# Row sums of late conditioning columns four products further on, and a fourth slot for mixed token tiles

## The chip, the cores and the metric

The kernel runs on one core of a Trainium2 chip. The metric is the device time of one execution, in microseconds (us). The engines are named as in the profile: PE is TensorE's matmuls and PEld its weight loads, DVE is VectorE, ACT is ScalarE, POOL is GpSimd, SP is the engine that issues most DMAs. Each engine works through its own instructions in order and waits on semaphores where it needs another's result; a queue of DMA issues is named SPq or ACTq.

## The reference

One layer of a bidirectional encoder: 1024 tokens, 1024 features, float32. Cut to what matters:

```python
mod = silu(c) @ w_ada + b_ada                      # six vectors of 1024: sh1 sc1 gt1 sh2 sc2 gt2
h = rms_norm(x, g_norm1) * (1 + sc1) + sh1
qa, ka, va, qb, kb, vb, gates = split(h @ w_in)    # 8 + 12 heads of 64, and two gates of 1024
o_a = neighbourhood_attention(rms(qa), rms(ka), va, rpb)
o_b = softmax-weighted sum of three dilated window attentions of (qb, kb, vb)
gate_a, gate_b = split(sigmoid(gates + b_gate))
x = x + gt1 * ((gate_a * (o_a @ w_proj_a) + gate_b * (o_b @ w_proj_b)) @ w_o)
h2 = rms_norm(x, g_norm2) * (1 + sc2) + sh2
a, up = split(h2 @ w_ffn_in)                       # 2 x 2816
x = x + gt2 * ((silu(a) * up) @ w_ffn_out)
```

The vectors sh1 and sc1 are made at the start. The other four make up 4096 "late" columns of the conditioning, in eight columns of 512: columns 0 to 3 are gt1 and sh2, 4 and 5 are sc2, 6 and 7 are gt2.

## The kernel before

**Precision and products.** Every float32 operand is split into a high and a low part (`hi`, made on ACT; `lo`, made on POOL or DVE), and each product takes three matmuls per step of the contraction: hi x hi, hi x lo, lo x hi (`PASS`). Large products are done in seven instead of eight block products, with mixed (added or subtracted) blocks of weights and of tokens. The mixed token blocks lie in DRAM as `t_d` (`TD` gives the four that are needed: x1, w22, x3, x2) and are loaded back when needed.

**Order.** TensorE's instructions run in the order in which the code writes them. On the other engines a scheduler may change the order; what the code wraps in `pin` keeps its order among the pinned instructions of its engine. Most loads for weights and all loads of mixed token tiles are pinned on SP. A load into a buffer waits, at the head of SP's queue, until the buffer's last reader is through.

**The paired projection (L1146 to L1253).** The input projection is made head pair by head pair (a "unit"). Units 4 to 9 are made two at a time by `pair_units`, which writes a list of blocks, `stream`. A block is one step of a product: three matmuls of 128 x 384. Four blocks make one token tile, four tiles one product, and the seven products p1, x1, p2, x2, x4, x3, w22 of a pair follow one another: 112 blocks for a pair, 336 for the three pairs, from block 192 on. A product starts at block `s`. `when(p, f)` puts a request ahead of block `p`: raw weights are asked for from `s - 29` on, their high parts are made from `s - 14` on, their low parts from `s - 12` on. Products x1, x2, x3 and w22 take their token tiles from `t_d` (`sload`, L1220). Attention for earlier units is put between the blocks by the main loop (L1265 to L1380), about once in seven blocks.

**Buffers of the pair stage.** The high and low parts of weights share one ring of ten buffers (`NHL`, tags hi and lo), and so do two of three mixed token tiles; each request takes the next buffer of the ring, and waits until the request ten places before it has been used up. A weight is used up by the product's fourth token tile. Every third mixed tile goes into a spare buffer, left free of the token tiles (`spare`, the profile calls it hT). Other buffers: `big` is a ring of eight large buffers for attention operands and others; acc2 holds a running sum of the early conditioning columns; rtab holds the rope table of units 0 to 5.

**The late conditioning columns (L342 to L369).** `late_ada` returns a function that does one step each time it is called. Steps 0 to 7 of a column load one 128 x 512 block of `wada2` and add it, scaled by the conditioning, to the column's sum (`acc`) on DVE. One step of the next column then sums over the 128 partitions: four small matmuls with `ones32` (L352), an add of the bias on DVE (L357) and a store to DRAM, `mod_d` (L358). The bias is loaded by SP ahead of the add (L356). One such function, `ada_gate`, does columns 4 and 5 in the late gate stage: it is called once behind each of the 24 products of `gate_group` (L1443 to L1456). The other, `ada_late`, does columns 6 and 7: it is called once in each of the last 20 of 22 passes of the feed-forward stage (L1811 to L1821). The vector gt2 is loaded from `mod_d` behind that stage (L1828).

**After the gate stage** come eight merges (`merge`, L1465), each of 36 matmuls, the product with `w_o`, the feed-forward input (22 passes of `pair_out`) and the feed-forward output (seven products of `prod2`, L1860). Banks of TensorE's results are given out in turns, two for each of four tags.

Of the kernel before, what the change touches and what calls it, by code (L numbers as in the profile page):

```python
# [11 lines left out]
F32R = mybir.dt.float32r  # L12
# [36 lines left out]
def hybrid_layer(ctx: ExitStack, tc: tile.TileContext, x, colp, wada1, wada2, bada2, wqkv, wg, wpa, wpb,  # L49
# [3 lines left out]
    def pool(name, side, **kw):  # L53
        return tc.alloc_tile_pool(name=name, bufs=1, side=side, reuse_waits="tile", **kw)
# [25 lines left out]
    def bank(tag):  # L80
        return ps.tile([128, 512], F32, tag=tag, name="ps_" + tag)
# [33 lines left out]
    def fview(ap):  # L115
        return ap.bitcast(F32)
# [37 lines left out]
    def spare(q, n, dtype=F32R):  # L154
        return (h1p, h1l)[q].tile([128, n], dtype, tag=f"h{q}01" + ("a" if n == 1536 else "b"), bufs=1, name="hT")
# [15 lines left out]
    ap_ = pool("attn", "right")  # L171
# [7 lines left out]
    def big(name, shape=None, dtype=F32):  # L179
        return ap_.tile(shape or wide, dtype, tag="big", bufs=NBIG, name=name)  # L180
# [27 lines left out]
    def unit_load(u, k, keep=False):  # L208
        return wload(wqkv[u, :, k, :], 384, keep)
# [66 lines left out]
    def tok(part, k, t):  # L276
        return hT[part][k // 4, t // 4][0][k % 4][:, t % 4 * 128:t % 4 * 128 + 128]

    rtab = []
# [62 lines left out]
    def late_ada(p, c0, bankf, tile):  # L342
        state, acc = [0], {}

        def step():
            i = state[0]
            state[0] += 1
            c, kk = c0 + i // 8, i % 8
            if kk == 1 and c0 < c <= c0 + 2:
                pm = bankf()  # L350
                for j in range(4):
                    nc.tensor.matmul(pm[32 * j:32 * j + 32, :128], ones32, acc[c - 1][:, 128 * j:128 * j + 128],  # L352
                                     start=True, stop=True)
                br = p.tile([128, 128], F32, tag="br", bufs=1, name="brow")
                bq = bada2[:, (c - 1) * 512:c * 512].rearrange("o (j n) -> (o j) n", j=4)
                nc.sync.dma_start(br, bq[:, None, :].to_broadcast([4, 32, 128]))  # L356
                nc.vector.tensor_add(br, pm[:, :128], br)  # L357
                nc.sync.dma_start(mod_d[(c - 1) * 512:c * 512].rearrange("(j n) -> j n", j=4), br[0:128:32, :])  # L358
            if i >= 16:
                return  # L360
            wa = tile()
            nc.sync.dma_start(wa, wada2[c, :, kk, :])
            if kk == 0:
                acc[c] = p.tile([128, 512], F32, tag="acc", bufs=2, name="acc3")
                nc.vector.tensor_scalar(acc[c], wa, cact[:, 0:1], None, op0=ALU.mult)
            else:
                nc.vector.scalar_tensor_tensor(acc[c], wa, cact[:, kk:kk + 1], acc[c], op0=ALU.mult, op1=ALU.add)

        return step  # L369
# [743 lines left out]
    def when(p, f):  # L1113
        events.setdefault(p, []).append(f)
# [33 lines left out]
    sums, nmix = [], [0]  # L1148
# [26 lines left out]
    def pair_units(ua):  # L1175
        ub = ua + 1
        chain, ch = [], {}
        for nm in PROD:
            s = len(stream)
            r, w = {}, {}  # L1180
            e, k0 = SRC[nm]
            for k in range(4):
                def load(k=k, nm=nm, r=r, e=e, k0=k0):
                    if nm == "x1":
                        if k % 2 == 0:
                            chain.append(big("chain"))
                        ch[k] = chain[-1][:, 512 * (k % 2):512 * (k % 2) + 384]
                        pin(nc.sync.dma_start(ch[k], wqkv[ub, :, k, :]))
                    r[k] = unit_load((ua, ub)[e], k0 + k, True)

                def mix(k=k, nm=nm, r=r):
                    if nm == "x1":
                        nc.gpsimd.tensor_add(ch[k], ch[k], r[k])
                    elif nm == "x2":
                        nc.gpsimd.tensor_sub(ch[k], ch[k], r[k])
                    elif nm == "x4":
                        nc.gpsimd.tensor_sub(r[k], r[k], ch[k])
                    elif nm == "x3":
                        nc.gpsimd.tensor_sub(ch[k], r[k], ch[k])

                def high(k=k, nm=nm, r=r, w=w, s=s):
                    z = ch[k] if nm in ("x1", "x2", "x3") else r[k]
                    w[k] = [wp.tile([128, 512], F32R, tag=g, bufs=NHL, name="w" + g) for g in ("hi", "lo")] + [z]
                    h = nc.scalar.activation(w[k][0][:, :384], z, AF.Copy)  # L1204
                    if s > 192:
                        pin(h)

                def low(k=k, w=w):
                    hi, lo, z = w[k]
                    nc.gpsimd.tensor_sub(lo[:, :384], z, fview(hi[:, :384]))  # L1210

                first = s == 192
                when(s - 29 + 3 * k, load)
                when(s - 19 + 2 * k, mix)
                when(s + (-14, -12, -6, -5)[k] if first else s - 14 + 2 * k, high)
                when(s + (-13, -11, -5, -4)[k] if first else s - 12 + 2 * k, low)
            for t in range(4):
                sm = {}
                if nm in TD:
                    def sload(t=t, nm=nm, sm=sm):  # L1220
                        nmix[0] += 1
                        for q, tag in enumerate(("hi", "lo")):
                            if nmix[0] % 3 == 0:
                                z = spare(q, 512)
                            else:
                                z = wp.tile([128, 512], F32R, tag=tag, bufs=NHL, name="smix")
                            pin(nc.sync.dma_start(fview(z).rearrange("p (k q) -> p k q", k=4), t_d[q, TD[nm], t]))
                            sm[q] = z

                    when(s - 15 + 3 * t if nm in ("x1", "x2", "x3") and t < 3 else s + 4 * t - 8, sload)  # L1230

                def job(k, t=t, nm=nm, w=w, sm=sm):
                    if k == 0:
                        n, i = now
                        sm["pd"] = bank("s" if n % 2 == 0 and n < PAIRED and 0 < i < 4 else "d")
                    pd = sm["pd"]
                    for i, (a, b) in enumerate(PASS):
                        if nm in TD:
                            lhs = sm[a][:, 128 * k:128 * k + 128]
                        else:  # L1240
                            lhs = tok(a, k + (0 if nm == "p1" else 4), t + (4 if nm == "x4" else 0))
                        nc.tensor.matmul(pd[:, :384], lhs, w[k][b][:, :384], start=(k == 0 and i == 0),  # L1242
                                         stop=(k == 3 and i == 2))
                    if k == 3:
                        pair_evac(nm, t, pd, ua, ub)

                for k in range(4):
                    stream.append(lambda k=k, job=job: job(k))
# [3 lines left out]
    for u in (4, 6, 8):  # L1252
        pair_units(u)  # L1253
# [11 lines left out]
    for n in range(6, 92):  # L1265
        u, t = divmod(n, 8)
# [455 lines left out]
    def first_prods(j):  # L1722
        wj[j, "p"] = prod(wj[j, "w11"], blk(0, 0)), prod(wj[j, "w12"], blk(1, 0))

    def first_out(j):
        p1, p2 = wj[j, "p"]
        c11, c12 = cs[j] = [half_tile("e", NE) for _ in range(2)]
        nc.scalar.activation(c12, p1, AF.Copy)
        nc.vector.tensor_add(c11, c12, p2)
# [22 lines left out]
    def first_back(j):  # L1752
        cs[j] = [half_tile("e", NE) for _ in range(2)]
        for n, z in enumerate(cs[j]):
            nc.sync.dma_start(z, e_d[EARLY.index(j) - HELD, n])
# [39 lines left out]
    ada_late = late_ada(adp, 6, prod_bank, lambda: adp.tile([128, 512], F32, tag="wa", bufs=3, name="wa3"))  # L1795
# [15 lines left out]
    for n, j in enumerate(EARLY + tuple(i for k in range(len(EARLY) // 2, HT) for i in (k, k + HT))):  # L1811
        if j not in EARLY[:2]:
            late_weights(j)
        if j in EARLY[HELD:]:
            first_back(j)
        elif j not in cs:
            first_prods(j)
            first_out(j)
        if n >= 2:
            ada_late()  # L1820
        pair_out(j)  # L1821
    for p in tps[::-1] + [ep]:
        p.release()
# [207 lines left out]
```

## Time and profile before

| | us |
|---|---|
| median of 3 runs | 1484.25 |
| lowest and highest run | 1483.57, 1489.17 |
| the profiled execution | 1483.4 |
| its span | 1481.6 |
| PE busy in the span | 1452.2 |
| DVE busy | 1103.0 |
| POOL busy | 731.7 |
| ACT busy | 706.4 |

The profile shows one execution. The page groups instructions by source line, engine and names (the name left of the arrow is written, those right of it are read). A list of waits says for which instruction another one waited, in total, how often and the longest. A timeline gives start, duration, engine, line and operation, and in brackets how long the engine had been idle and who ended that. The windows view gives the busy time of the engines in a stretch and the clock that TensorE was granted, as a share of full speed.

In time the stages lie so: up to about 197 us the start and units 0 to 3, with attention; about 197 to 480 the three pairs; to 608 the first gate products; 608 to 688 the gate groups with `ada_gate`; then the merges, the output projection, the feed-forward input to about 1266 and the feed-forward output.

### The profile page before, as it was taken

Reading aid. Unit: us, or ns where it says so; the run is one execution under the profiler, and the core shown is the slowest. Engines: PE = TensorE matmul, PEld = TensorE weight load, DVE = VectorE, ACT = ScalarE, POOL = GpSimd, SP = SyncE. Lnnn points to the kernel's source line nnn. Section 1 sums busy time; section 2 is a strip of 40 time slices with the busy share of each in tenths; the row PEclk is TensorE's granted clock in tenths of the full one; section 3 lists DMA queues with packets and bytes.
Section 4 is the critical chain, followed back from the end, with each engine's and each line's share of the span. In section 5 each row is a group of like instructions: output and inputs, shape, how many; then the busy total and the mean of one; then the engine's idle time right before and its main releaser. Section 6 shows DMA issues by size and latency. Waiting matters only on the chain.

```text
span 1481.6 us, 24516 instructions
## 1 busy us (share of the span) xinstructions
PE 1452.2 (98%) x8024; PEld 1236.5 (83%) x8024; DVE 1103.0 (74%) x2120; ACT 706.4 (48%) x1771; POOL 731.7 (49%) x706
## 2 busy tenths in 40 slices
PE   8999999998999999989999999999999999999998
PEld 7999999898887777867888888888888888888886
DVE  6788857767588765794877596888777777599568
ACT  5666666656777764545422353332233233354442
POOL 0453476663544464445531402677777775104464
PEclk9999999999999999999999999999999999999999
DMA  9657685756667776955374325345533334898342
GB/s 361 240 175 237 200 276 171 241 181 207 218 185 239 239 247 208 375 159 167 121 247 150 105 87 178 122 152 175 175 102 107 106 109 143 272 349 304 114 157 100
DMA packets 191569, 285.18 MB, mean 192 GB/s; under 512 B 29745, under 2 KB 91857, under 8 KB 190673
## 3 DMA queue, kind: packets, MB, share of 16 engines
q1 hardware_dynamic: 172864, 269.96, 54.6%
q10 hardware_dynamic: 18576, 13.64, 2.8%
q8 instruction: 64, 1.05, 0.3%
q14 instruction: 65, 0.52, 0.1%
HBM read 218.67 MB, written 64.86 MB: 191 GB/s over the span
## 4 chain that ended last, share of the span: by engine, by line
PE 85%; DVE 7%; DMA 3%; ACT 2%; issue 2%; POOL 1%; SPq 0%; ACTq 0%; DVEq 0%; POOLq 0%
PE ps_v L1689 8%; PE ps_d L1689 8%; PE ps_s L1689 7%; PE ps_d L379 7%; PE ps_t L1689 6%; PE ps_d L880 5%; PE ps_d L1242 5%; PE ps_s L1866 3%; PE ps_d L1866 3%; PE ps_t L1866 3%; PE ps_v L1866 3%; PE ps_s L1624 2%; PE ps_d L1624 2%; PE ps_s L1242 2%; PE ps_v L1624 1%
## 5 line engine op out<-in xcount | busy, mean ns | idle before, releaser
L129 ACT ACTIVATE whi<-raw 128x512 fp32r<-128x512 f32 (+2 forms) x265 | 158.1, 609 | 193.9 <-PE ps_s L1866 37.9
L132 DVE TENSOR_TENSOR wlo<-raw,whi 128x512 fp32r<-128x512 f32 (+1 forms) x171 | 152.5, 909 | 47.9 <-ACT whi L129 45.4
L132 POOL TENSOR_TENSOR wlo<-raw,whi 128x512 fp32r<-128x512 f32 (+2 forms) x94 | 129.1, 1382 | 108.9 <-ACT whi L129 104.6
L379 PE MATMUL ps_d<-whi,hT 128*128 128x384 f32 x384 | 101.2, 338 | 0.0
L1639 POOL TENSOR_TENSOR e<-e,c 128x512 f32<-128x512 f32 x44 | 68.8, 1565 | 62.3 <-DVE c L1769 38.2
L1242 PE MATMUL ps_d<-whi,hT 128*128 128x384 f32 x328 | 92.1, 342 | 3.4 <-issue 1.6
L129 ACT ACTIVATE whi<-ws 128x512 fp32r<-128x512 f32 x60 | 37.7, 628 | 119.5 <-DVE ws L1706 81.2
L880 PE MATMUL ps_d<-hT,whi 128*128 128x512 f32 x264 | 84.2, 400 | 0.0
L132 POOL TENSOR_TENSOR wlo<-m,whi 128x512 fp32r<-128x512 f32 x35 | 51.5, 1479 | 51.0 <-ACT whi L129 51.0
L379 PEld LDWEIGHTS ps_d<-whi,hT 128*128 128x128 f32 x384 | 69.6, 188 | 0.6 <-issue 0.6
L1242 PE MATMUL ps_d<-whi,smix 128*128 128x384 f32 x224 | 65.8, 350 | 3.4 <-DMA smix<-t_d 3.1
L1210 POOL TENSOR_TENSOR wlo<-raw,whi 128x384 fp32r<-128x384 f32 x48 | 49.3, 1040 | 36.8 <-ACT whi L1204 32.3
L1637 ACT ACTIVATE e<-e 128x512 f32<-128x512 f32 x44 | 27.4, 630 | 81.8 <-DVE e L1772 56.3
L658 ACT ACTIVATE P<-P,st 128x256 f32<-128x256 f32 (+2 forms) x100 | 45.8, 460 | 38.9 <-DVE st L656 38.9
L379 PE MATMUL ps_d<-wlo,hT 128*128 128x384 f32 x192 | 64.2, 334 | 0.0
L1242 PEld LDWEIGHTS ps_d<-whi,hT 128*128 128x128 f32 x328 | 59.8, 188 | 4.9 <-issue 2.1
L1689 PE MATMUL ps_d<-h2T,whi 128*128 128x512 f32 x200 | 61.6, 389 | 0.0
L1689 PE MATMUL ps_v<-h2T,whi 128*128 128x512 f32 x192 | 59.2, 389 | 0.0
L1689 PE MATMUL ps_s<-h2T,whi 128*128 128x512 f32 x192 | 59.1, 389 | 0.0
L1210 POOL TENSOR_TENSOR wlo<-chain,whi 128x384 fp32r<-128x384 f32 x36 | 38.1, 1071 | 41.8 <-ACT whi L1204 39.4
L132 POOL TENSOR_TENSOR wlo<-gl,whi 128x512 fp32r<-128x512 f32 x30 | 41.2, 1389 | 33.5 <-ACT whi L129 33.4
L1638 DVE TENSOR_TENSOR e<-e 128x512 f32<-128x512 f32 x44 | 42.5, 974 | 17.0 <-ACT e L1637 16.8
(479 smaller groups left out, 4635.5 us busy)
## 6 DMA issues: line engine op xcount, KB each, us to landing
raw<-in_w_dram SPq DMA_DIRECT2D x139, 256.0 KB, 3.3
raw<-in_wqkv_dram SPq DMA_DIRECT2D x116, 192.0 KB, 4.1
ga_d<-e SPq DMA_DIRECT2D x77, 256.0 KB, 2.2
raw<-ga_d SPq DMA_DIRECT2D x77, 256.0 KB, 2.9
smix<-t_d SPq DMA_DIRECT2D x64, 256.0 KB, 3.7
m<-in_w_dram SPq DMA_DIRECT2D x44, 256.0 KB, 5.5
hT<-t_d SPq DMA_DIRECT2D x40, 256.0 KB, 4.3
xt<-in_x_dram SPq DMA_DIRECT2D x16, 512.0 KB, 7.1
```

Of the source, the lines that this page charges most:

```text
L129: h = nc.scalar.activation(hi[:, :n], r, AF.Copy)
L132: (eng or nc.gpsimd).tensor_sub(lo[:, :n], r, fview(hi[:, :n]))
L379: nc.tensor.matmul(pd[:, :384], tok(a, k, t), U.w[k][b][:, :384], start=(k == 0 and i == 0), stop=(k == KT - 1 and i == 2))
L658: nc.scalar.activation(C.P[h][:nq, c], C.P[h][:nq, c], AF.Exp, scale=-1.0, bias=nm, accum_out=sm)
L880: nc.tensor.matmul(pb, w[x][:, k * 128:(k + 1) * 128], b[y][k], start=(k == 0 and q == 0), stop=(k == 3 and q == 2))
L1210: nc.gpsimd.tensor_sub(lo[:, :384], z, fview(hi[:, :384]))
L1242: nc.tensor.matmul(pd[:, :384], lhs, w[k][b][:, :384], start=(k == 0 and i == 0), stop=(k == 3 and i == 2))
L1624: nc.tensor.matmul(pbs[hf], h2T[a][:, k, t * 128:(t + 1) * 128], wow[hf, k][b], start=(n == 0 and (a, b) == PASS[0]), stop=(n == KT - 1 an ...
L1638: nc.vector.tensor_mul(sg, sg, a)
L1639: nc.gpsimd.tensor_mul(sg, sg, up)
L1689: nc.tensor.matmul(pb, w[p][:, k * 128:(k + 1) * 128], b[q][:, k], start=(k == 0 and i == 0), stop=(k == 3 and i == 2))
L1866: nc.tensor.matmul(pb[m], o[0][a][:, m * 128:(m + 1) * 128], o[1][b], start=(k == 0 and i == 0), stop=(k == HT - 1 and i == 2))
```

## The change

Three edits. In `late_ada` the row sum of a column comes at step 5 of the next column instead of step 1, and the upper limit on its column is dropped. `ada_late` is called in all 22 passes instead of the last 20. In `sload` the mixed token tiles have four places in turn instead of three: two in the ring, the spare buffer, and a fourth, which is a `big` buffer in the first pair and the buffers acc2 and rtab in the other two; and all tiles of x1, x2 and x3 are asked for from 15 blocks ahead of their product, three blocks apart (before, the fourth tile 8 blocks ahead of its use), those of w22 12 blocks ahead of their use (before 8).

```diff
@@ -346,7 +346,7 @@
             i = state[0]
             state[0] += 1
             c, kk = c0 + i // 8, i % 8
-            if kk == 1 and c0 < c <= c0 + 2:
+            if kk == 5 and c > c0:
                 pm = bankf()
                 for j in range(4):
                     nc.tensor.matmul(pm[32 * j:32 * j + 32, :128], ones32, acc[c - 1][:, 128 * j:128 * j + 128],
@@ -1218,16 +1218,22 @@
                 sm = {}
                 if nm in TD:
                     def sload(t=t, nm=nm, sm=sm):
+                        slot = nmix[0] % 4
                         nmix[0] += 1
+                        if slot == 3 and ua == 4:
+                            pair = big("smix", [128, 2, 512], F32R)
                         for q, tag in enumerate(("hi", "lo")):
-                            if nmix[0] % 3 == 0:
+                            if slot == 2:
                                 z = spare(q, 512)
+                            elif slot == 3:
+                                z = pair[:, q] if ua == 4 else ap_.tile([128, 512], F32R, tag=("acc2", "rtab")[q], bufs=1,
+                                                                        name="smix")
                             else:
                                 z = wp.tile([128, 512], F32R, tag=tag, bufs=NHL, name="smix")
                             pin(nc.sync.dma_start(fview(z).rearrange("p (k q) -> p k q", k=4), t_d[q, TD[nm], t]))
                             sm[q] = z
 
-                    when(s - 15 + 3 * t if nm in ("x1", "x2", "x3") and t < 3 else s + 4 * t - 8, sload)
+                    when(s + 4 * t - 12 if nm == "w22" else s - 15 + 3 * t, sload)
 
                 def job(k, t=t, nm=nm, w=w, sm=sm):
                     if k == 0:
@@ -1816,8 +1822,7 @@
         elif j not in cs:
             first_prods(j)
             first_out(j)
-        if n >= 2:
-            ada_late()
+        ada_late()
         pair_out(j)
     for p in tps[::-1] + [ep]:
         p.release()
```

## The prediction

> **What bounds the kernel now.** I read the page first, then the windows view over the stages, the list of TensorE's waits, the windows view again around the longest waits (for the granted clock), and the timelines of the queues there.
>
> ```profile
> span 1481.6 us, 24516 instructions
> ...
> PE 1452.2 (98%) x8024; PEld 1236.5 (83%) x8024; DVE 1103.0 (74%) x2120; ACT 706.4 (48%) x1771; POOL 731.7 (49%) x706
> ```
>
> ```profile
> 196.50:480.00 283.50, 272.98 (x2012) 247.75 (x2009) 204.28 (x661) 187.53 (x618) 158.26 (x206) 0.99 0.68 213
> ...
> 608.00:688.00 80.00, 72.62 (x322) 58.88 (x321) 62.28 (x73) 41.45 (x66) 41.49 (x29) 0.96 0.65 227
> ...
> 870.00:1266.00 396.00, 396.00 (x1760) 327.19 (x1759) 304.36 (x361) 125.23 (x214) 252.59 (x176) 1.00 0.41 134
> ```
>
> The columns are length, then busy time of PE, PEld, DVE, ACT and POOL, granted clock, DMA share, GB/s. TensorE is the bound: 98% of the span, and all of 870 to 1266. What can be won is the time in which it stands or runs with a lowered clock. Both show in the two stages that the change touches: the paired projection (196.5 to 480, 10.5 us not busy, clock 0.99) and the late gate products (608 to 688, 7.4 us not busy, clock 0.96).
>
> ```profile
> PE ps_t L352 <- DVE acc L367: 4.6, 1, 4.6
> PE ps_d L1242 <- DMA smix<-t_d: 3.1, 3, 2.5
> PE ps_s L352 <- DVE acc L367: 2.8, 1, 2.8
> ...
> PE ps_s L1242 <- DMA hT<-t_d: 1.7, 1, 1.7
> PE ps_d L1242 <- issue: 1.6, 1, 1.6
> ...
> PE ps_s L1242 <- DVE st L656: 1.0, 1, 1.0
> PE ps_d L1242 <- DVE sx L596: 1.0, 1, 1.0
> ...
> PE ps_d L1242 <- DMA hT<-t_d: 0.6, 1, 0.6
> ```
>
> Total, times, longest. Two row sums (L352) waited 4.6 and 2.8 = 7.4 us for the VectorE sums of their columns. Products on mixed tokens waited 3.1 + 1.7 + 0.6 = 5.4 us for loads ("hT" from t_d is a mixed tile in the spare slot). The rows that name DVE st, DVE sx and issue are waits that no token load ends; the change does not aim at them.
>
> ```profile
> 638.00:641.00 3.00, 0.24 (x5) 1.00 0.78 216
> 641.00:645.00 4.00, 4.00 (x24) 1.00 0.96 253
> 663.00:668.00 5.00, 0.39 (x5) 0.86 0.00 2
> 668.00:671.00 3.00, 3.00 (x14) 0.50 0.01 3
> 671.00:674.00 3.00, 3.00 (x10) 0.59 0.77 273
> ...
> 279.50:282.00 2.50, 2.46 (x10) 0.79 1.02 337
> 282.00:285.50 3.50, 3.50 (x15) 0.66 1.04 352
> ...
> 368.20:374.00 5.80, 5.39 (x22) 0.71 1.04 276
> ```
>
> PE alone; the number behind the count is the clock. A wait can cost twice. After the 4.6 us wait TensorE ran at 0.50 and 0.59 for 6 us; after the 1.7 us wait (ending at 279.5) at 0.79 and 0.66 for 6 us; after the 2.5 us wait (ending at 368.2) at 0.71 for 5.8 us. After the 2.8 us wait (ending at 641) it stayed at 1.00.
>
> **Part A: row sums of the late columns, gate stage.** The step runs once behind each of 24 gate products. Steps 0 to 7 and 8 to 15 build two sums on VectorE; their four row-sum matmuls move from behind products 9 and 17 to behind 13 and 21.
>
> ```profile
> 639.40 1.50 DVE L367 SCALAR_TENSOR_TENSOR acc<-wa,cact,acc 128x512 f32<-128x512 f32 x2
> ...
> 640.96 0.43 PE L352 MATMUL ps_s<-acc,ones 128*32 128x128 f32 x8 [2.76 <-DVE acc L367]
> ...
> 667.17 0.76 DVE L367 SCALAR_TENSOR_TENSOR acc<-wa,cact,acc 128x512 f32<-128x512 f32 x1
> 667.98 0.66 PE L352 MATMUL ps_t<-acc,ones 128*32 128x128 f32 x8 [4.61 <-DVE acc L367]
> ...
> 673.69 0.62 PE L880 MATMUL ps_d<-hT,whi 128*128 128x512 f32 x2
> ...
> 673.89 0.69 DVE L1449 TENSOR_TENSOR sg<-sg,ps_v 128x512 f32<-128x512 f32 x1 [4.57 <-PE ps_v L880]
> ...
> 676.41 0.62 PE L880 MATMUL ps_s<-hT,whi 128*128 128x512 f32 x2
> ```
>
> A product takes 676.41 - 673.69 = 2.72 us. The second sum ended at 667.9. TensorE had come to its row sum at 667.98 - 4.61 = 663.4; four products later is 663.4 + 10.9 = 674.3, less the 2.8 us that the first wait no longer takes: 671.5, 3.6 us after the sum. The first has 638.2 + 10.9 = 649.1 against 640.9. So both waits go: 4.61 + 2.76 = 7.4 us. With the second goes its slow clock: 3 x 0.50 + 3 x 0.41 = 2.7 us. VectorE was 4.57 us idle before 673.89, so its backlog was worked off by 669; it is not a second bound that takes the gain back.
>
> What is moved, and past what: on PE the four matmuls, past four products each; on VectorE the add of the bias, past four adds of those products; on SP the bias load and the store into mod_d, past the loads of the same four steps. POOL and ACT have no part in it.
>
> ```profile
> SPq L358 <- DVE brow L357: 10.8, 1, 10.8
> ```
>
> SP stood 10.8 us before that store, with attention tiles and the first merge weights behind it in the code's order. Behind step 21 the code has only loads for the third merge and later. I cost the store at nothing; the cover is two merges of 36 matmuls, 2.72 / 12 us apart: 16 us. With the cover gone, at most the 10.8 us would come back.
>
> In the feed-forward stage the step starts two passes earlier; row sums come at passes 13 and 21 of 22 instead of 11 and 19.
>
> ```profile
> L367 DVE SCALAR_TENSOR_TENSOR acc<-wa,cact,acc x28: 715/752/2970, 606.2 to 792.3; 128x512 f32<-128x512 f32 x28
> ```
>
> All sums were done by 793, before the stage began at 870, so nothing waits there before or after. The last column's result is stored two passes later (396 / 22 = 18 us each), in the last pass, and is first used after four output products of 11 x 2.72 us. Zero; the cover is 120 us, and without it the cost would be the store's landing, a few us.
>
> **Part B: a fourth slot, earlier requests.** Counted from the code: paired products run in blocks of three matmuls, four blocks to a token tile, seven products of 16 blocks to a pair. Weights and most mixed tiles take turns in a ring of ten buffers; every third mixed tile has the spare slot. A request waits at the head of SP's queue until the buffer's last user is through. Before, the first and second w22 tiles of a pair get their buffer as little as 3 and 6 blocks before use, those in the spare slot 8, and eight of the weight requests stand 5 to 7 blocks for a buffer. After, no weight request stands; x1, x2 and x3 tiles find a buffer long free and are asked 15 to 18 blocks ahead; w22 tiles have 17, 7, 12 and 12 blocks from buffer to use. The last three of these requests still come up to five blocks before their buffer is free; behind them in SP's queue stand the next pair's weights, for which ACT, POOL and then PE would wait.
>
> ```profile
> DMA to landing us min/median/max: 2.9/3.7/6.2
> ```
>
> ```profile
> 356.74 0.33 PE L1242 MATMUL ps_d<-whi,smix 128*128 128x384 f32 x1
> ...
> 362.57 0.35 PE L1242 MATMUL ps_d<-whi,hT 128*128 128x384 f32 x1
> ...
> 368.26 0.41 PE L1242 MATMUL ps_d<-whi,smix 128*128 128x384 f32 x1 [2.52 <-DMA smix<-t_d]
> ```
>
> ```profile
> 363.88 0.32 SPq L466 DMA_DIRECT2D v<-v_d  x1
> 364.29 0.86 SPq L1227 DMA_DIRECT2D smix<-t_d  x2
> ```
>
> The 2.5 us wait: issued at 364.29 behind the load of v, needed at 365.7, landed at 368.2. The new request lies four blocks earlier, ahead of that v load. Its buffer is free at 356.74, where the fourth x3 tile starts: 9 us for 0.9 us of issue and 3.7 of landing. Tightest is the second w22 tile, free one block after 356.74 (357.3) and used at 362.57: 5.3 us against 4.6. With the slowest landing (6.2) it would wait 1.8 us, 5.4 over three pairs; that is the upper bound, and I take zero because the median fits. So the 5.4 us of load waits go, and the lowered clock behind them: 2.5 x 0.21 + 3.5 x 0.34 + 5.8 x 0.29 = 3.4 us.
>
> [...]
>
> The eight weight requests go from standing to not standing; no row above shows PE waiting for them, so I count zero. Next late are the waits for VectorE: without the pauses VectorE falls further behind, and I put back one wait of the size of the DVE rows, 1.0 us; gone altogether, the rows of 1.6 + 1.0 + 1.0 would add 3.6 us of gain.
>
> The new buffers: in the first pair a large attention buffer, later the acc2 and rope-table buffers.
>
> ```profile
> 293.36 0.26 POOL L435 TENSOR_TENSOR rb<-qn,rtab 128x32 f32<-128x32 f32 x1
> ```
>
> That is the rope table's last use, about where the fourth x1 tile of the next pair is asked, 18 blocks before it is needed. Zero.
>
> **Sum.** The profiled execution took 1483.4 us, 1.8 around its span and 0.85 under the median of 1484.25. 1483.4 - 7.4 - 2.7 - 5.4 - 3.4 + 1.0 = 1465.5; against the median 1466.
>
> **Rivals.**
> Clock not tied to the short waits: the low clock at 280 and 370 comes with DMA shares of 1.04, and the 2.8 us wait lowered nothing. 3.4 us stay: 1469.4. Against: it begins right behind each wait. Chance 0.12.
> Only A: waits move to the second w22 tile, or the loads land later in these DMA-full stretches (1.02, 1.04). 1484.25 - 10.1 = 1474. For: 5.3 against 4.6 us. Chance 0.13.
> Only B: in the gate stage VectorE (62.3 of 80 us busy) becomes the bound and late weights take the place of the row sum. 1484.25 - 8.8 = 1475.4. Against: the idle 4.57 us. Chance 0.08.
> It doesn't do what it says: sums end later still and loads stand at the same places: 1484. Chance 0.05.
> Slower: SP stands before w22 loads whose buffers are not free and holds the next pair's weights.
>
> ```profile
> SPq L1227 <- PE ps_d L1242: 56.5, 24, 9.4
> ```
>
> It stood 9.4 us once. By the code the weights behind have 9 blocks from the second w22 buffer to their split, at 283.5 / 336 = 0.84 us a block 7.6 us; less a landing of 3.7 that leaves 3.9. If each pair stood 9.4 us longer there, TensorE would wait 5.5 us and lose 3 more at half clock: 26 us on three pairs, 1466 + 26 = 1492. It decides from 3.9 us on. Against: that stand ends after 5 blocks by the count. Chance 0.04.
> [...]
>
> **How the numbers follow.** My forecast has the other 0.58, its own range 1460 to 1471 (3.6 more gain and 2 of sums read off windows below; the late w22 tile above). A measurement here can tell 0.5%, 7.4 us, so faster is under 1476.8: forecast and first three rivals, 0.91, less 0.09 for the parts of the two near the limit that come out above it: 0.82. Same: 0.05 + 0.09 = 0.14. Slower: 0.04. The range 1460 to 1478 leaves out the last two rivals and a tail, some 0.15.
>
> **What would show it.** L352 without a DVE wait near 640 and 665; clock 1.00 from 608 to 688, that stage 10 us shorter; no DMA smix or hT row above 1 us on L1242; clock 1.00 from 196 to 480, 8 us shorter. Wrong if L352 still waits for acc, if L880 waits for DVE wlo, or if the pair stage keeps its length with SP standing on L1227.

## The result and the profile after

| | before | after |
|---|---|---|
| median, us | 1487.44 | 1472.38 |
| lowest and highest run of after, us | | 1468.93, 1475.41 |
| ratio, 95% interval | | 0.9904 [0.9883, 0.9926] |
| the profiled execution, us | 1483.4 | 1472.6 |

The kernel became faster by 1%. The column of before has six runs, the three of the first table and 1486.83, 1488.05 and 5082.91, so its median is not the 1484.25 of the first table. The ratio is taken from the fast runs alone, without that of 5082.91. The ratio times 1484.25 is 1470, 14.2 us less; the forecast was 1466, 18 us less.

The page of the changed kernel begins so:

```profile
span 1470.8 us, 24489 instructions
...
PE 1449.9 (99%) x8024; PEld 1235.4 (84%) x8024; DVE 1102.8 (75%) x2120; ACT 703.9 (48%) x1771; POOL 732.5 (50%) x706
```

The work is the same on every engine; only TensorE's share of the span rose, from 98 to 99%. Lines from 1224 to 1818 of before are numbered six higher (L1242 is now L1248, L1624 is L1630, L1478 is L1484). The windows of the stages, with the columns of the prediction:

```profile
196.50:480.00 283.50, 274.19 (x2041) 249.85 (x2040) 212.38 (x666) 189.79 (x626) 166.59 (x213) 0.99 0.69 219
608.00:688.00 80.00, 80.00 (x365) 65.45 (x364) 62.96 (x77) 41.19 (x67) 47.30 (x33) 1.00 0.69 234
870.00:1260.00 390.00, 390.00 (x1732) 321.91 (x1731) 295.32 (x347) 122.01 (x213) 253.95 (x177) 1.00 0.42 137
```

The late gate products (608 to 688) run without a gap and at clock 1.00, where before 7.4 us were not busy and the clock was 0.96. The pair stage still has 283.50 - 274.19 = 9.3 us in which TensorE stands, against 10.5, and its clock is again 0.99. The two row sums of the gate stage, in TensorE's timeline, wait for nothing (a wait would stand in brackets behind the row):

```profile
646.37 0.43 PE L352 MATMUL ps_s<-acc,ones 128*32 128x128 f32 x8
668.71 0.43 PE L352 MATMUL ps_t<-acc,ones 128*32 128x128 f32 x8
```

The list of TensorE's waits (total, times, longest), those in the start and of 0.2 left out, and one of 0.6 for VectorE (L477) behind the pair stage:

```profile
PE ps_s L579 <- DVE qk L506: 3.0, 1, 3.0
...
PE ps_d L1630 <- DVE sg L1484: 1.3, 1, 1.3
PE ps_t L605 <- ACT P L597: 1.3, 1, 1.3
PE ps_d L1248 <- DVE hT L1169: 1.1, 1, 1.1
PE ps_t L301 <- DVE PT L678: 1.0, 1, 1.0
PE ps_s L1248 <- DVE st L656: 1.0, 1, 1.0
...
PE ps_d L1248 <- DVE rz L415: 0.9, 1, 0.9
...
PE ps_d L1248 <- DMA smix<-t_d: 0.6, 2, 0.3
PE ps_d L1248 <- PE ps_d L1248: 0.5, 2, 0.3
```

Of 5.4 us of waits for mixed tiles 0.6 are left. In their place stand waits for VectorE: 3.0 + 1.1 + 1.0 + 1.0 + 0.9 = 7.0 us in the pair stage. In the kernel before these were st 1.0 and sx 1.0, shown in the prediction, and four more rows of its list:

```profile
PE ps_d L1242 <- DVE rz L416: 0.4, 1, 0.4
PE ps_s L579 <- DVE qk L506: 0.3, 1, 0.3
PE ps_t L301 <- DVE PT L678: 0.3, 1, 0.3
...
PE ps_d L1242 <- DVE hT L1169: 0.2, 1, 0.2
```

Together 3.2 us. So in the pair stage VectorE took back 3.8 us. A new row for ACT (L605, 1.3) stands against the row "issue" of 1.6, which is gone.

**Where the new 3.0 us wait comes from.** The timelines of POOL, DVE and PE of the changed kernel, in order of time:

```profile
465.91 3.75 POOL L132 TENSOR_TENSOR wlo<-raw,whi 128x512 fp32r<-128x512 f32 x3 [0.47 <-ACT whi L129]
...
467.26 1.20 DVE L416 SCALAR_TENSOR_TENSOR rz<-rz,rv 128x8 f32<-128x8 f32 x1
468.38 0.42 DVE L505 SCALAR_TENSOR_TENSOR qk<-ps_v,hg,qk 128x128 fp32r<-128x128 f32 x1
468.72 1.56 DVE L426 SCALAR_TENSOR_TENSOR qn<-qn,rz 128x256 f32<-128x256 f32 x2
470.20 0.36 DVE L506 TENSOR_TENSOR qk<-ps_v,qk 128x128 fp32r<-128x128 f32 x1
...
470.62 0.80 PE L579 MATMUL ps_s<-qk 64*128 64x256 f32 x4 [3.03 <-DVE qk L506]
```

TensorE needs `qk`, which L505 and L506 make. Two L426 stand between them, and these and L416 are slow as long as POOL works on three weight tiles, from 465.91 to 469.66. In the kernel before POOL did the same tiles at 469.13, and the two L426 came behind them:

```profile
469.13 3.78 POOL L132 TENSOR_TENSOR wlo<-raw,whi 128x512 fp32r<-128x512 f32 x3 [0.33 <-ACT whi L129]
...
473.39 0.15 DVE L416 SCALAR_TENSOR_TENSOR rz<-rz,rv 128x8 f32<-128x8 f32 x1
...
473.80 0.74 DVE L426 SCALAR_TENSOR_TENSOR qn<-qn,rz 128x256 f32<-128x256 f32 x2
```

There L416 took 0.15 us and the two L426 0.74, against 1.20 and 1.56 beside POOL's work. Taken singly, POOL's first two tiles end at 467.20 and 468.43, and L415 and L416, begun while they ran, end at 467.22 and 468.46: each of VectorE's two ends only when the tile does that POOL was at. L416 and L426 read two tiles that both lie in SBUF. L505, one of whose operands is a bank of TensorE's results (`ps_v`), took 0.42 beside POOL's work, and 0.43 away from it (at 465.48 in the kernel before). That the overlap is what costs here is read from these times; POOL's work was not moved away to try it. And VectorE's order is not that of the kernel before: there L505 and L506 stood together, ahead of the two L426, so not all of the 3.0 us need be lag.

Behind the wait the clock falls again (PE alone, as in the prediction):

```profile
471.00:474.00 3.00, 3.00 (x22) 0.50 1.03 335
474.00:475.00 1.00, 1.00 (x8) 0.99 1.03 360
```

**The new wait at 740 us.** L1630 is the first line of the output projection, L1484 the addition with which VectorE empties a bank of the merges. TensorE's and VectorE's timelines of the changed kernel:

```profile
739.93 0.84 PE L1630 MATMUL ps_d<-wr,h2T 128*128 128x512 f32 x3
741.39 0.67 DVE L1484 TENSOR_TENSOR sg<-sg,ps_d 128x512 f32<-128x512 f32 x1
742.12 1.20 PE L1630 MATMUL ps_d<-wr,h2T 128*128 128x512 f32 x4 [1.35 <-DVE sg L1484]
```

TensorE, no longer held up by the row sums, is through the merges before VectorE is. Before there was no such row.

**By stage.** Each stage is taken from its line's first matmul in the timeline to the next one's (gate, merge and output projection: from the end of the one to the end of the next), so these times do not depend on what went before; each is good to about 0.2 us:

| us | first plain product at | units 1 to 3 | pairs | gate | merges | output projection | feed-forward input | rest |
|---|---|---|---|---|---|---|---|---|
| before | 59.7 | 139.2 | 280.9 | 207.3 | 65.2 | 92.4 | 421.9 | 215.0 |
| after | 62.6 | 139.2 | 277.4 | 195.2 | 65.3 | 94.0 | 422.1 | 215.0 |

The pairs won 3.5 us, the gate stage 12.1, and the output projection gave 1.6 back: 14.0 us, which agrees with the ratio. The two profiled executions differ by only 10.8, because the start, which the change does not touch, was shorter in the profile of before than in any other (60.5 to 63.3 us in the other executions profiled). The stage's first rows in the timelines of before and after:

```profile
59.70 0.33 PE L379 MATMUL ps_t<-whi,hT 128*128 128x384 f32 x1
```

```profile
62.65 0.33 PE L379 MATMUL ps_t<-whi,hT 128*128 128x384 f32 x1
```

### The profile page after: what moved, and what is told of

Same layout as the page of the kernel before. It is cut to its first block, busy times and chain, and to the rows that moved or that the text cites. A ratio compares the mean times of both kernels' runs of the same rounds, so it can differ in the third digit from the quotient of the medians.

```text
span 1470.8 us, 24489 instructions
## 1 busy us (share of the span) xinstructions
PE 1449.9 (99%) x8024; PEld 1235.4 (84%) x8024; DVE 1102.8 (75%) x2120; ACT 703.9 (48%) x1771; POOL 732.5 (50%) x706
## 4 chain that ended last, share of the span: by engine, by line
PE 48%; DVE 3%; ACT 1%; DMA 1%; issue 0%; POOL 0%; SPq 0%; ACTq 0%; DVEq 0%
PE ps_s L1695 8%; PE ps_d L1695 7%; PE ps_v L1695 7%; PE ps_t L1695 6%; PE ps_s L1871 4%; PE ps_d L1871 4%; PE ps_t L1871 3%; PE ps_v L1871 3%; PE ps_s L1630 2%; PE ps_d L1630 2%; PE ps_v L1630 1%; DVE sg L1485 1%; DVE wlo L132 1%; DMA sg<-sig_d 1%; ACT h2T L1486 1%; DVE sg L1484 0%
## 5 line engine op out<-in xcount | busy, mean ns | idle before, releaser
L132 DVE TENSOR_TENSOR wlo<-raw,whi 128x512 fp32r<-128x512 f32 (+1 forms) x171 | 148.9, 888 | 50.1 <-ACT whi L129 47.0
L379 PE MATMUL ps_d<-whi,hT 128*128 128x384 f32 x384 | 101.3, 338 | 0.0
L1248 PE MATMUL ps_d<-whi,hT 128*128 128x384 f32 x312 | 88.1, 342 | 1.3 <-DVE hT L1169 1.1
L1248 PE MATMUL ps_d<-whi,smix 128*128 128x384 f32 x240 | 68.1, 343 | 0.9 <-DMA smix<-t_d 0.6
L1248 PEld LDWEIGHTS ps_d<-whi,hT 128*128 128x128 f32 x312 | 57.0, 188 | 2.4 <-DVE hT L1169 1.4
L1695 PE MATMUL ps_d<-h2T,whi 128*128 128x512 f32 x184 | 56.7, 390 | 0.0
```

The costliest lines, as they stand in the source:

```text
L132: (eng or nc.gpsimd).tensor_sub(lo[:, :n], r, fview(hi[:, :n]))
L379: nc.tensor.matmul(pd[:, :384], tok(a, k, t), U.w[k][b][:, :384], start=(k == 0 and i == 0), stop=(k == KT - 1 and i == 2))
L1695: nc.tensor.matmul(pb, w[p][:, k * 128:(k + 1) * 128], b[q][:, k], start=(k == 0 and i == 0), stop=(k == 3 and i == 2))
```

## The experiments

The theory after the result: part A (the row sums) gives nearly what was forecast; part B (the tiles) takes the load waits away, but VectorE's waits come in their place, since it has no less work and loses the pauses in which it caught up. This reason is argued; each edit also gives VectorE another order, and after_qk, quad200 and quad_pair ask how much that does. The rivals are named with each run. Ratios are to the kernel before, with the 95% interval of the runs in turn with it on the same chip.

| kernel | ratio | pairs, us | gate, us | output projection, us |
|---|---|---|---|---|
| the change | 0.9904 [0.9883, 0.9926] | 277.4 | 195.2 | 94.0 |
| a_only | 0.9925 [0.9907, 0.9942] | 281.5 | 197.6 | 94.0 |
| b_only | 0.9941 [0.9925, 0.9957] | 277.0 | 203.9 | 92.4 |
| slot_only | 0.9991 [0.9977, 1.0005] | 281.3 | 207.0 | 92.4 |
| early_only | 0.9956 [0.9943, 0.9970] | 277.5 | 210.4 | 92.4 |
| row3 | 0.9920 [0.9903, 0.9937] | 278.1 | 199.8 | 92.4 |
| row2 | 0.9952 [0.9934, 0.9971] | 278.0 | 207.0 | 92.4 |
| after_qk | 0.9899 [0.9879, 0.9919] | 276.5 | 195.2 | 94.0 |
| quad200 | 0.9902 [0.9886, 0.9918] | 273.3 | 200.6 | 94.7 |
| quad_pair | 0.9914 [0.9900, 0.9927] | 277.7 | 199.5 | 93.8 |
| mpool | 0.9894 [0.9880, 0.9907] | 275.1 | 194.5 | 92.8 |
| quad_pair_mpool | 0.9913 [0.9900, 0.9927] | 278.6 | 196.6 | 92.4 |
| qk_mpool | 0.9899 [0.9885, 0.9914] | 279.2 | 198.2 | 92.8 |

**a_only: the row sums alone.** The kernel before with the first and the last hunk of the diff:

```diff
-            if kk == 1 and c0 < c <= c0 + 2:
+            if kk == 5 and c > c0:
...
-        if n >= 2:
-            ada_late()
+        ada_late()
```

> The row sums alone are moved (and the late step runs in all 22 feed-forward passes); the token tiles have their three places as before. Theory: the gate stage gives its 7.4 us of waits and 2.7 us of lowered clock by itself, so the stage (first gate product to first merge) goes from 207 to 195-197 us, the pair stage stays at 281, and the time is 10 to 12 us under before, ratio 0.992 to 0.993. Rival (most of the gain is the token tiles'): ratio above 0.996.

The gate stage is 207.3 - 197.6 = 9.7 us shorter, against 10.1 forecast, and no row sum waits. But the output projection is 1.6 us longer, with this row in the list of TensorE's waits:

```profile
PE ps_d L1624 <- DVE sg L1478: 1.3, 1, 1.3
```

It stands in neither the kernel before nor in those of the runs below whose row sums are early.

**b_only: the tiles alone.** The changed kernel with the row sums of before:

```diff
-            if kk == 5 and c > c0:
+            if kk == 1 and c0 < c <= c0 + 2:
...
-        ada_late()
+        if n >= 2:
+            ada_late()
```

> The fourth slot and the earlier requests alone; row sums as before. Theory: the load waits (5.4 us) and the slow clock behind them (3.4 us) go, and a new wait of 3.0 us with 1.7 us of slow clock behind it, at the pair stage's end, takes half of it back: pair stage 277 to 278 us against 281, gate stage 207 as before, time 3 to 5 us under before, ratio 0.9965 to 0.998. Rival (whatever load wait is removed comes back as VectorE waits): ratio 0.999 to 1.001, pair stage 280 or more.

The ratio lies below the expected 0.9965 to 0.998. The pairs are 3.9 us shorter instead of 7.8, and the gate stage is shorter by 3.4 as well, which was not expected: VectorE's order differs, the two row sums wait 5.0 and 0.3 us instead of 2.8 and 4.6, and a wait of 1.8 at 491 us (L477 for VectorE) is gone. In TensorE's timeline:

```profile
641.31 0.63 PE L352 MATMUL ps_s<-acc,ones 128*32 128x128 f32 x8 [4.96 <-DVE acc L367]
665.62 0.43 PE L352 MATMUL ps_t<-acc,ones 128*32 128x128 f32 x8 [0.33 <-DVE acc L367]
```

So B's total is near the forecast by another sum, and it overlaps A's: part A would have taken those row-sum waits anyway.

**slot_only and early_only: B's two halves.** The kernel before with the fourth slot alone (the third hunk's places, the request times as before), and with the new request times alone:

```diff
-                    when(s - 15 + 3 * t if nm in ("x1", "x2", "x3") and t < 3 else s + 4 * t - 8, sload)
+                    when(s + 4 * t - 12 if nm == "w22" else s - 15 + 3 * t, sload)
```

> The fourth slot alone, the requests at their old distances (w22 tiles and each fourth tile 8 blocks ahead). Theory (it is the distance that removes the load waits): w22 tiles still come late, DMA waits of 2 to 5 us on L1248 remain in all, time about as before, ratio 0.998 to 1.001. Rival (it is the freed ring places): no DMA wait above 1 us, the same time as with the earlier requests, ratio 0.9965 to 0.998.

> The new request times of the mixed tiles without the fourth slot, and without the later row sums. By the rotation of the buffers, counted from the code, the tightest tile then has 6 blocks from buffer to use instead of 3, but SP stands for buffers in 21 requests instead of 12, up to 10 blocks (8.4 us) at a time. Theory (the request times bring the gain, the slot only keeps SP's queue free): waits of TensorE for mixed tiles in the pair stage fall from 5.5 to under 1.5 us in all, the pair stage is 276.5 to 278.5 us, ratio 0.993 to 0.996. Rival 1 (the slot is needed as well): those waits stay at 3 us or more, pair stage 280 to 282, ratio 0.998 to 1.001. Rival 2 (the slower rival of the prediction: SP stands before buffers and holds the next weights): waits for weight tiles appear, in rows that name POOL wlo, ACT whi or DMA w on L1242, pair stage 283 or more, ratio over 1.001.

With the slot alone the waits for mixed tiles remained, though smaller, and those for VectorE were up without any gain:

```profile
PE ps_d L1248 <- DVE hT L1169: 2.4, 1, 2.4
PE ps_s L1248 <- DVE st L656: 2.0, 2, 1.2
PE ps_d L1248 <- DMA smix<-t_d: 1.8, 2, 1.5
```

With the request times alone the waits for tiles fell to 0.4 us and the pairs to 277.5, as with the whole of B; SP's list shows the price that the prediction's slower rival named. The first fence is early_only, the second the changed kernel:

```profile
SPq L1227 <- PE ps_d L1242: 72.0, 18, 10.5
```

```profile
SPq L1233 <- PE ps_d L1248: 29.3, 10, 7.5
```

SP stood up to 10.5 us and 72 us in all, against 9.4 and 56.5 in the kernel before, and no row of TensorE's waits in the pair stage names a weight tile. So the slot only keeps SP's queue free; the gain in the pairs comes from asking earlier. The slower rival did not come; its 3.9 us counted extra standing ahead of the next pair's weights, and which of these stands are extra there was not followed up. TensorE's waits for VectorE in this pair stage are 4.5 us, not the 7.0 of the changed kernel, with as few load waits: how much VectorE takes back depends on its order too. The gate stage of early_only is 3.1 us longer than before, with row-sum waits of the same 2.8 and 4.5 us; behind the first of them the clock fell to 0.50, which it had not done before (below), and what else is in it was not followed up. The profiled execution is also the slowest of the nine (1484.21, median 1479.72), so its stages do not add up to the ratio.

**row3 and row2: how late must the row sums be?**

```diff
-            if kk == 5 and c > c0:
+            if kk == 3 and c0 < c <= c0 + 2:
```

and the same with `kk == 2`.

> The changed kernel with the row sums three products behind their sums instead of five. In the changed kernel the two sums of the gate stage end at 640.6 and 665.7 and the row sums come at 646.4 and 668.7; two products of 2.72 us earlier is 640.9 and 663.3. Theory (VectorE lags by two to four products, and the place must cover the longer lag): the first row sum waits at most 0.3 us, the second about 2.4; gate stage 197.5 to 198.5 us against 195.2, or 200 if the clock is lowered behind it; ratio to the changed kernel's 0.990: about 0.992 to 0.994. Rival (any place past the first products will do, since VectorE catches up at once): no wait, gate stage 195.2, ratio 0.990.

> The changed kernel with the row sums two products behind their sums. One product earlier than with three: TensorE comes to them at 638.2 and 660.5 and waits 2.4 and then, since the first wait gives VectorE no less work, 2.7 us more. Theory: two waits of 2 to 3 us each, gate stage 200 to 202 us if the clock stays at 1.00 behind waits under 3 us, 202 to 204 if it falls as it did behind the load waits of 1.7 and 2.5 us of the kernel before; ratio 0.994 to 0.996. Rival (the row sums' places do not matter from two products on): gate stage 195 to 197, ratio 0.990.

TensorE's rows of row3, then of row2:

```profile
639.99 0.43 PE L352 MATMUL ps_v<-acc,ones 128*32 128x128 f32 x8
665.21 0.43 PE L352 MATMUL ps_d<-acc,ones 128*32 128x128 f32 x8 [2.80 <-DVE acc L367]
```

```profile
638.90 0.43 PE L352 MATMUL ps_t<-acc,ones 128*32 128x128 f32 x8 [2.35 <-DVE acc L367]
668.06 0.65 PE L352 MATMUL ps_v<-acc,ones 128*32 128x128 f32 x8 [5.15 <-DVE acc L367]
```

At three products the first wait is gone and the second is 2.8 us, as the theory had it. At two products the second is 5.2 instead of 2.7, and the gate stage has the 207 us of the kernel before, more than the 200 to 204 expected. VectorE's lag is between three and five products for the second sum; the place that the change chose covers it, and the rival (any place will do) fell.

**after_qk: the two L426 taken from between L505 and L506**, at 470 us alone. The scheduler's precedence for these two instructions is raised there, which puts L506 ahead of the two L426; nothing else in the order of TensorE, VectorE, ACT or POOL differs in the trace:

```diff
-                with tc.high_priority(off):
+                with tc.high_priority(off() if callable(off) else off):
...
-    @urgent(QT)
+    @urgent(lambda: 200 if 72 <= now[0] <= 75 else QT)
```

> The changed kernel with one pair of VectorE instructions swapped: at the end of the pair stage the low part of k (L506) stands ahead of two scalings (L426) instead of behind them; nothing else in any queue differs. Theory: the 3.0 us wait of the scores (L579) for L506 and the clock of 0.66 for 5 us behind it go, pair stage 273 instead of 277.5, time 4 to 5 us under the changed kernel, ratio to before 0.987 to 0.988. Rival (VectorE is behind by a fixed amount of work and TensorE meets it at the next place): a wait of 2 to 3 us on VectorE within the next 10 us, pair stage 276 or more, ratio 0.990.

The wait at 470 us fell from 3.0 to 1.5 us, and the pairs won 0.9 instead of some 4; waits for st L656 rose from 1.0 to 2.4, and all waits for VectorE in the pair stage come to 7.4 us against 7.0. So what was won at one place was met again at others, as the rival had it. The time cannot be told from that of the changed kernel.

**quad200 and quad_pair: the same precedence everywhere** (`PP, QT, AQ, AT, AV = 100, 200, 0, 0, 0`), and from pass 56 to 75 of the order alone (`200 if 56 <= now[0] <= 75 else QT`).

> The changed kernel with the rotations of q and k (L505, L506) put ahead on VectorE everywhere, not only at 470 us. Theory (what is left in the pair stage is VectorE's lag, 6.9 us of waits that name it, and its amount of work does not change): the wait for qk at 470 us goes, others come in its place; pair stage 275.5 to 278, ratio 0.988 to 0.992. Rival (the order on VectorE alone makes these waits): the waits that name VectorE fall under 4 us in all, pair stage 272 to 274, ratio under 0.988. It may also be slower, where other work waits for the operations that are put behind.

> The changed kernel with L505 and L506 put ahead on VectorE in the pair stage alone (four places; 40 lines of difference in VectorE's order, none in the gate stage, where the kernel with this everywhere gave 1.6 + 0.9 us of waits and 3.4 us of slow clock back). Theory (those waits came from the order in the other places): pair and gate stage together 469 to 471 us against 472.6 in the changed kernel, ratio 0.987 to 0.989. Rival (VectorE has the same work, the waits come somewhere else): together 471.5 to 474, ratio 0.990.

In quad200 the pairs took 273.3 us, which was the rival's number, but the waits there that name VectorE are 6.3 us and not under 4, and pairs and gate stage together took 473.9, against 472.6 in the changed kernel: what the pairs won comes back in the gate stage (200.6 us against 195.2), at whose beginning TensorE's list has this row:

```profile
PE ps_v L620 <- DVE PT L609: 1.7, 1, 1.7
```

quad_pair was meant to leave that place alone, and has the same 1.7 us wait there; together 477.2, more than theory or rival had (its profiled execution is the slowest of the five). The orders tried on VectorE move these waits; they do not remove them.

**mpool: less work for VectorE in the merges.** In the changed kernel:

```diff
-            nc.vector.tensor_sub(h2T[1][:, i, hs], m, fview(h2T[0][:, i, hs]))
+            (nc.gpsimd if i >= 5 else nc.vector).tensor_sub(h2T[1][:, i, hs], m, fview(h2T[0][:, i, hs]))
```

> The changed kernel with the last subtraction of the last three merges (L1487, six of 128x512, 0.69 us each on VectorE) on POOL; every other queue is as in the changed kernel. Theory (with the row sums out of the way TensorE comes to the output projection 1.4 us before VectorE has read the merge's banks, so part A's gain is cut there by VectorE): 6 x 0.69 = 4.1 us less on VectorE, the wait L1630 <- DVE sg L1484 of 1.3 us goes, that stage is 92.4 us instead of 94.0, ratio to the changed kernel's about 0.999. Rival (POOL, which works there on weights with 1.3 us a tile, becomes late, or slows VectorE's own work as at 470 us): the wait stays or one for POOL on h2T or wlo takes its place; stage 94 to 98 us.

The row for L1630 is gone and the output projection takes 92.8 us instead of 94.0. So that stage's loss is VectorE's, as the theory said. The gain of 1.2 us is too small for the interval: 0.9894 lies within the changed kernel's. Its pair stage of 275.1 is run variation; nothing ahead of the merges was edited, and the order of the engines there is the same.

**quad_pair_mpool and qk_mpool: two edits together.**

> Both edits in one kernel. If both theories hold: pair and gate stage together 469 to 471 us, output projection's stage 92.4, about 4 us less than the changed kernel, ratio 0.986 to 0.988. If neither: 0.990, as the changed kernel.

> The two single edits of the changed kernel that helped a stage, together: L505 and L506 one after the other on VectorE at 470 us (wait for qk 3.0 to 1.5 us), and the last merges' L1487 on POOL (no wait at the output projection's start). Theory (both waits are VectorE's, in places that do not touch): pair stage 275 to 276.5 us, gate 194.5 to 195.5, output projection 92.4 to 92.8, ratio 0.987 to 0.989, with the clock's share by chance: none, one or two stretches of 3.4 us at 0.50 behind the 1.5 us wait, 1.7 us each. Rival (VectorE's lag returns in other places): 0.990 as the changed kernel.

The output projection has its 92.4 and 92.8 us in both; the pairs and the gate stage did not add up (475.2 and 477.4 together). None of the six versions beside the changed kernel can be told from it: their ratios lie between 0.9894 and 0.9914, all inside its interval. I found no version that beats it beyond doubt.

**The clock, over the runs.** In the pair and gate stages of the kernel before and of the changed kernel the clock was at 0.50 for 3.41 us or for 6.82, so 1.7 or 3.4 us were lost each time. PE alone, in the kernel before:

```profile
280.94:284.35 3.41, 3.41 (x12) 0.50 1.03 347
369.69:373.10 3.41, 3.41 (x16) 0.50 0.97 220
666.65:673.47 6.82, 5.49 (x20) 0.50 0.28 99
```

and in the changed kernel:

```profile
470.61:474.02 3.41, 3.40 (x23) 0.50 1.03 341
```

Which of them follows a wait is not told by its length. The wait for L506 is 3.0 us in the changed kernel and in mpool, in the same place. In the first the clock was at 0.50 for 3.4 us; in mpool it was low for 6.8 us; by timeline and window, PE alone:

```profile
466.24 0.80 PE L579 MATMUL ps_s<-qk 64*128 64x256 f32 x4 [3.01 <-DVE qk L506]
```

```profile
466.00:472.00 6.00, 5.76 (x29) 0.50 0.98 332
```

In quad200 the wait there is half as long and cost nothing, with the clock at 1.00 behind it (busy times of all five engines):

```profile
465.82 0.51 PE L579 MATMUL ps_s<-qk 64*128 64x256 f32 x4 [1.54 <-DVE qk L506]
```

```profile
465.00:471.00 6.00, 5.18 (x43) 4.57 (x43) 4.49 (x17) 2.25 (x9) 1.34 (x2) 1.00 1.00 345
```

In qk_mpool the same wait is as short, and the clock fell behind it (PE alone):

```profile
470.49 0.65 PE L579 MATMUL ps_s<-qk 64*128 64x256 f32 x4 [1.55 <-DVE qk L506]
```

```profile
471.50:474.00 2.50, 2.50 (x19) 0.50 1.05 331
```

The row sum's wait of 2.8 us left the clock at 1.00 in the kernel before (prediction); in row3 and in early_only the same length was followed by these windows:

```profile
665.50:668.50 3.00, 3.00 (x15) 2.35 (x8) 2.25 (x5) 1.66 (x3) 3.00 (x3) 0.50 0.19 55
```

```profile
640.00:644.00 4.00, 4.00 (x16) 2.94 (x17) 0.77 (x2) 2.14 (x3) 1.27 (x1) 0.50 0.96 260
```

A high DMA share was not there each time: it was 0.19 in row3's window, and 0.28 from 666.65 on in the kernel before. What sets the waits that cost clock apart from those that cost none is not shown; no run was made to find it.

## Why the prediction was right, and where it was off

The direction, the range and the two mechanisms held: 1470 by the ratio, in a range of 1460 to 1478, against a forecast of 1466. Point by point:

- **Row sums, 7.4 us, and the clock behind them, 2.7.** Right in every part of "what would show it" for this stage: no wait at 646 and 669, clock 1.00. a_only gave 9.7 of 10.1 in the gate stage, and row3 and row2 show that one or two products later is too little; three later was not run.
- **"It is not a second bound that takes the gain back."** Wrong by 1.6 us. The idle 4.57 us before 673.89 was read as a sign that VectorE had caught up, and so it had at that point; but it had been idle because TensorE stood. Without that wait it runs late through the merges, and TensorE meets it at 740. a_only shows the wait with A alone, row3 and row2 show it gone when TensorE is held up by 2.8 us or more, and mpool shows it gone when VectorE has 4.1 us less to do.
- **Load waits, 5.4 us.** Right: 0.6 left with all of B, 0.4 with the request times alone. The upper bound of 5.4 us for the late w22 tiles was not needed.
- **"I put back one wait of the size of the DVE rows, 1.0 us."** This is the term that was mis-sized. Waits for VectorE in the pair stage rose from 3.2 to 7.0, by 3.8 us, and one of them, 3.0 us long, brought 1.7 us of slow clock (0.50 from 470.61 to 474.02), so that of the 3.4 us that were to come back only 1.7 did: 3.8 + 1.7 = 5.5 us in all, where 1.0 was set down. The pairs won 3.5 instead of 7.8, and the sign "clock 1.00 from 196 to 480, 8 us shorter" did not come.
- **Clock.** The prediction tied the slow clock to the waits, and in that it was right; its windows of 0.79, 0.66 and 0.71 are two stretches of 3.41 us at 0.50, from 280.94 and from 369.69. Why the wait of 2.8 us lowered nothing, the rival's ground, is not shown; in row3 and early_only a wait as long was followed by 0.50. The rival of 1469 (short waits not tied to the clock) gives nearly the measured time, but for another reason: new waits, not the old clock.
- **Not foreseen, in its favour:** the gate stage won 12.1, not 10.1. That is luck. b_only shows the source: the wait of 1.8 us at 491 us went too.
- **SP's queue.** The prediction had the weights at risk from 3.9 us of extra standing. In the changed kernel SP stood 29.3 us for these buffers, against 56.5 before, and the rival did not come; early_only stood 15.5 us more than before and no weight came late, but whether any stand ahead of the weights was 3.9 us longer is not shown. The count that x2 and x3 tiles find a buffer long free was off: in the third pair the second x2 tile stood 7.5 us and the second x3 tile 7.1 us for TensorE, at no cost to it.

The sum: 17.9 forecast, less 4.3 in the pairs, less 1.6 at the output projection, plus 2.0 in the gate stage makes 14.0. So the forecast is as near as it is partly because the 2.0 us stand against the other two.

## What to carry to other kernels

When the longest engine is idle for a second engine's work or for loads, the pauses are also what lets a third engine keep up: with that engine at 75% of the span, price what it may take back from the trace (here 3.8 us of waits for 4.8 us of load waits removed, but 1.3 for 7.4 of row sums), and look for it stages later too, at the next place where a bank or tile must be handed over. Ask earlier for what is late before adding buffers, and measure both halves apart: here the request times alone carried the pairs' gain. A matmul that sums up another engine's work belongs as many products behind it as that engine lags, which here was more than three.

## What the runs showed of the hardware that was not expected

- In the kernel before and in the changed kernel a lowered clock cost 1.7 or 3.4 us a time, at 0.50 for 3.41 or 6.82 us. Waits of 1.5 to 3.0 us for the same L506 were followed by none of it in quad200 (1.54 us), by 3.4 us of it in qk_mpool (1.55) and in the changed kernel (3.03), and by 6.8 in mpool (3.01). Single profiles of the pair stage differ by some 2 us without any edit there (277.4 in the changed kernel, 275.1 in mpool).
- VectorE's small operations on two tiles in SBUF took up to 1.20 us instead of 0.15 (L416, 128x8, at 467.26 in the changed kernel and at 473.39 in the kernel before) while POOL worked on weight tiles of 128x512, and POOL's own three tiles took 3.75 us there and 3.78 in the kernel before, where L416 and L426 came behind them: only VectorE was slowed. In the traces of these two kernels L426 (128x256) took 0.41 to 0.43 us each outside POOL's work and up to 1.52 within it; L506 on 128x128, with one operand in a bank, took 0.35 to 0.41 in either case.
